# Ten gate and up pairs by seven products instead of nine, with the first pair's inputs and weight sums made earlier, in a two-layer encoder on one core

## The chip, the cores and the metric

The kernel runs on one core of one Trainium2 chip. TensorE (PE) multiplies, VectorE (DVE) and ScalarE (ACT) do elementwise work, GpSimd (POOL) issues accumulating transfers and takes powers, SyncE (SP) issues most other transfers. The time is the device time of one execution in microseconds, the median of several runs.

## The reference

Two layers over 512 tokens of 1024 channels, all in float32: layer 0 with latent attention, layer 1 with chunked attention over a shared key and value band. Each is followed by the feed-forward block that the change is about:

```python
def swiglu(h, w_gate, w_up, w_down):
    return (jax.nn.silu(h @ w_gate) * (h @ w_up)) @ w_down

for layer in range(DEPTH):
    h = rms_norm(x, attn_pre_g[layer])
    ...
    x = x + rms_norm(y, attn_post_g[layer])
    h = rms_norm(x, ffn_pre_g[layer])
    f = swiglu(h, ffn_w_gate[layer], ffn_w_up[layer], ffn_w_down[layer])
    x = x + rms_norm(f, ffn_post_g[layer])
```

`w_gate` and `w_up` are 1024 x 2816, `w_down` is 2816 x 1024.

## The kernel before, in words

**Halves.** Every float32 operand of a matmul is split into a high and a low half (`split`, L143: ScalarE casts the high half at L144, VectorE subtracts for the low half at L145), and each product is three matmuls: high by high, high by low, low by high. Weights arrive in `raw` buffers (512 KB, a ring of five) and their halves stand in `whi` and `wlo`, rings of three. `Feed` (L264) holds the plan of all weight pieces in order; `feed.next` hands out a piece and splits the next ones ahead.

**Blocks of the hidden layer.** The 2816 hidden units are 22 blocks of 128. A block's gate and up outputs stand transposed, hidden units on partitions and 512 tokens in the free dimension. The first `N_WHOLE` blocks, called whole units here, are multiplied plainly. Four whole units: the first two (weights `w_gu0`) in two halves of the tokens, so that they can begin while the second half of x is still made (`half`, L1153, four banks); units 2 and 3 (weights `w_gu`) on all 512 tokens by `proj` (L382, matmuls at L377 to L379).

**Pairs by seven products.** The other 18 blocks go in nine pairs (`products`, L1520, matmuls at L1550). For a pair, the weights of two blocks and two halves of the tokens make a 2 by 2 by 2 product, which is done with seven products instead of eight. Product j multiplies one of seven weight pieces (1024 columns: 4 quarters of the depth for gate and up) by one of seven moving operands of 256 tokens. Four of the seven pieces are sums of others, `raw[0]`, `raw[3]`, `raw[4]`, `raw[6]` (`Pair`, L151), made by accumulating transfers from POOL (L171) or by VectorE (L184). The moving operands are halves of x itself (`xs`, products 1, 2, 6) and sums of scaled x, here x-sums (`tb`, products 0, 3, 4, 5), made by `blocks_of` (L1315) once for all pairs. The results stand in the banks `be`, `al`, `ga` and are put together by ScalarE copies and VectorE adds; then the norm's factor (`rb`), silu (L1568) and the product with up follow.

**The order around it.** `ffn` (L1134) is the block: `out_proj` (L687) is the attention's output product, also in two halves of tokens; `Post.apply` (L667) adds the normed result to x, first half 0, then half 1 (y times a factor at L672, x plus y at L674, halves of x at L148 and L149). Behind each half stand its sums of squares for the next norm (`sx.squares`, L457 to L463), summed over channels by four transposing matmuls (L473). x of the layer is fetched ahead of `out_proj` (L683), and `mid` keeps x for later. In layer 1, `by_tokens` turns the result of layer 0 for the last stage, a piece in each of the products 0, 1, 3 and 5 from the second pair on. A scheduler puts each engine's instructions in order by dependences and by `behind` (issue after a named instruction) and `first` (priority); each engine then runs its queue strictly in order.

## Time and profile before

| | us |
|---|---|
| median of 3 runs | 1105.39 (1103.52 to 1105.41) |
| the profiled execution | 1105.07 |
| its span in the trace | 1103.3 |

The lines that matter are quoted in the prediction. In a line of the timeline the first number is the start in us from the begin of the span, the second how long it took, and in brackets stands the idle time before it and what ended that. In a group of instructions stand the count, the busy time in us, the mean of one in ns and the idle time just before. Names such as `whi<-raw` are output and input.

The costliest groups of the two elementwise engines:

```profile
L144 ACT CAST whi<-raw 128x1024 fp32r<-128x1024 f32 (+3 forms) x220 | 221.0, 1006 | 205.6 <-PE al L1550 71.5
L145 DVE TENSOR_TENSOR wlo<-raw,whi 128x1024 fp32r<-128x1024 f32 (+3 forms) x220 | 255.8, 1164 | 67.1 <-ACT whi L144 66.1
```

### The profile page before, as it was taken

How to read it: one execution, taken by the hardware profiler on the slowest of the kernel's cores; microseconds unless marked ns; L12 is line 12 of the kernel's file. 1: busy time of each engine (PE TensorE's matmuls, PEld its weight loads, DVE VectorE, ACT ScalarE, POOL GpSimd, SP SyncE). 2: the span in 40 equal slices, each digit the busy share in tenths (PEclk: the TensorE clock that was granted, in tenths of full speed). 3: DMA queues.
4: the chain of work that ended last, by engine and by line, in shares of the span. 5: the costliest groups of instructions: out<-in, count | busy, mean ns of one | idle time of the engine just before them, and what ended most of it. 6: DMA issues, size and time to landing. Idle time of an engine off the chain costs nothing.

```text
span 1103.3 us, 19079 instructions
## 1 busy us (share of the span) xinstructions
PE 1092.4 (99%) x6893; PEld 978.8 (89%) x6893; DVE 908.5 (82%) x1659; ACT 678.3 (61%) x1323; POOL 117.1 (11%) x181
## 2 busy tenths in 40 slices
PE   9999999999999999999999999999999999999997
PEld 6887889999999998888888888889899999998885
DVE  7787747988878889978858898758988889789977
ACT  7575737655555556668636767657645555556675
POOL 2211100101000001500000110000100010001401
PEclk9999999999999999999999999999999999999999
DMA  7344226447787757961555677634638888758913
GB/s 240 120 116 142 62 68 238 143 116 184 171 202 184 180 167 248 164 191 49 190 153 156 173 192 186 168 121 161 198 103 214 228 207 223 216 178 249 171 29 76
DMA packets 88334, 181.47 MB, mean 164 GB/s; under 512 B 26816, under 2 KB 28608, under 8 KB 88240
## 3 DMA queue, kind: packets, MB, share of 16 engines
q1 hardware_dynamic: 74752, 147.10, 43.1%
q0 software_dynamic: 13056, 32.73, 16.4%
q8 instruction: 54, 0.88, 0.3%
q10 hardware_dynamic: 432, 0.44, 0.1%
q14 instruction: 40, 0.33, 0.1%
HBM read 148.88 MB, written 10.88 MB: 145 GB/s over the span
## 4 chain that ended last, share of the span: by engine, by line
PE 97%; DVE 1%; ACT 1%; issue 1%; DMA 0%; POOL 0%; DVEq 0%; POOLq 0%; SPq 0%; ACTq 0%
PE al L1550 19%; PE b L377 11%; PE b L378 11%; PE b L379 11%; PE be L1550 9%; PE al L1306 8%; PE be L1306 5%; PE ga L1550 5%; PE de L1306 3%; PE ga L1306 3%; PE pt L561 2%; PE b L1707 2%; PE b L1107 1%; PE sc L1699 1%; PE sc L1698 1%
## 5 line engine op out<-in xcount | busy, mean ns | idle before, releaser
L144 ACT CAST whi<-raw 128x1024 fp32r<-128x1024 f32 (+3 forms) x220 | 221.0, 1006 | 205.6 <-PE al L1550 71.5
L145 DVE TENSOR_TENSOR wlo<-raw,whi 128x1024 fp32r<-128x1024 f32 (+3 forms) x220 | 255.8, 1164 | 67.1 <-ACT whi L144 66.1
L1550 PE MATMUL al<-th,whi 128*128 128x256 f32 x432 | 122.8, 284 | 0.0
L1550 PE MATMUL al<-th,wlo 128*128 128x256 f32 x432 | 121.0, 280 | 0.0
L1550 PE MATMUL al<-tl,whi 128*128 128x256 f32 x432 | 121.0, 280 | 0.0
L377 PE MATMUL b<-xh,whi 128*128 128x512 f32 x234 | 96.7, 415 | 0.0
L378 PE MATMUL b<-xl,whi 128*128 128x512 f32 x234 | 91.8, 392 | 0.0
L379 PE MATMUL b<-xh,wlo 128*128 128x512 f32 x234 | 91.7, 392 | 0.0
L1550 PEld LDWEIGHTS al<-th,whi 128*128 128x128 f32 x432 | 81.3, 188 | 2.2
L1550 PEld LDWEIGHTS al<-th,wlo 128*128 128x128 f32 x432 | 81.3, 188 | 0.2 <-DVE wlo L145 0.2
L1550 PEld LDWEIGHTS al<-tl,whi 128*128 128x128 f32 x432 | 81.3, 188 | 0.0
L548 ACT ACTIVATE p<-p,mn 128x128 f32<-128x128 f32 (+1 forms) x96 | 54.1, 563 | 36.0 <-DVE mn L546 34.1
L145 DVE TENSOR_TENSOR ptl<-pt,pth 128x128 fp32r<-128x128 f32 (+1 forms) x96 | 46.6, 485 | 30.5 <-ACT pth L144 29.6
L145 DVE TENSOR_TENSOR wlo<-wd,whi 128x512 fp32r<-128x512 f32 x86 | 56.3, 684 | 14.6 <-ACT whi L144 14.4
L144 ACT CAST whi<-wd 128x512 fp32r<-128x512 f32 x86 | 49.8, 618 | 25.0 <-PE al L1306 10.7
L144 ACT CAST pth<-pt 128x128 fp32r<-128x128 f32 (+1 forms) x96 | 40.3, 422 | 32.2 <-PE pt L561 31.3
L171 POOL DMA_DIRECT2D raw<-in_w_pair x32 | 28.1, 895 | 285.9 <-DVE ut L1562 84.1
L379 PEld LDWEIGHTS b<-xh,wlo 128*128 128x128 f32 x234 | 43.9, 188 | 9.9 <-DVE wlo L145 0.3
L1306 PE MATMUL al<-whi,pl 128*128 128x512 f32 x132 | 51.5, 390 | 0.0
L1306 PE MATMUL al<-wlo,ph 128*128 128x512 f32 x132 | 51.4, 389 | 0.0
L1306 PE MATMUL al<-whi,ph 128*128 128x512 f32 x132 | 51.4, 389 | 0.0
L377 PEld LDWEIGHTS b<-xh,whi 128*128 128x128 f32 x234 | 44.2, 189 | 5.7 <-ACT whi L144 0.2
(320 smaller groups left out, 3391.2 us busy)
## 6 DMA issues: line engine op xcount, KB each, us to landing
raw<-in_w_pair SPq DMA_DIRECT2D x88, 512.0 KB, 4.6
raw<-in_w_pair POOLq DMA_DIRECT2D x32, 512.0 KB, 7.6
wd<-in_w_down SPq DMA_DIRECT2D x54, 256.0 KB, 6.0
raw<-in_w_o SPq DMA_DIRECT2D x16, 512.0 KB, 4.0
raw<-in_w_gu SPq DMA_DIRECT2D x16, 512.0 KB, 4.7
raw<-in_w_down SPq DMA_DIRECT2D x16, 512.0 KB, 4.3
raw<-in_w_qkb SPq DMA_DIRECT2D x16, 512.0 KB, 3.5
wd<-in_w_down POOLq DMA_DIRECT2D x22, 256.0 KB, 5.0
```

The costliest lines, as they stand in the source:

```text
L144: return (nc.scalar.copy(dst_hi, src), V.tensor_tensor(dst_lo, src, dst_hi.bitcast(F32), op=OP.subtract))
L145: V.tensor_tensor(dst_lo, src, dst_hi.bitcast(F32), op=OP.subtract))
L171: nc.gpsimd.dma_start(r[j], self.src[n], accum_op=OP.add)
L377: nc.tensor.matmul(o, l[0], r[0], start=start, stop=False)
L378: nc.tensor.matmul(o, l[0], r[1], start=False, stop=False)
L379: last_mm[0] = nc.tensor.matmul(o, l[1], r[0], start=False, stop=stop)
L548: nc.scalar.activation(p[:, :n], p[:, :n], AF.Exp, bias=mn[:, :1], scale=-1.0, accum_out=self.sums[:, qt:qt + 1])
L561: nc.tensor.transpose(t[:, kt * P:(kt + 1) * P], p[:, kt * P:(kt + 1) * P], ident)
L1107: nc.tensor.matmul(o[:, q_], va[kt][:, part, v_], pt[:, kt, q_], start=n + kt == 0, stop=n == 2 and kt == NQT - 1)
L1306: nc.tensor.matmul(to[e], l[c], r[d], start=j < 4 and k == 0 and n == 0, stop=k == NF // 2 - 1 and n == 2, skip_group_check=True)
L1550: nc.tensor.matmul(o, l[c], r[d], start=first_ and n == 0, stop=k == K2 - 1 and n == 2, skip_group_check=True)
L1707: nc.tensor.matmul(o[:, q_], vv, pt[:, kt, q_], start=pt is pth and kt == 0, stop=pt is ptl and kt == NQT - 1)
```

## The change

`N_WHOLE` goes from 4 to 2: the whole units 2 and 3 and their weights `w_gu` go, and a tenth pair stands in their place, at the head of the pairs. The first pair now begins right behind the two whole units. Beside that:

- It runs its products in the order 1, 2, 0, 3, 6, 4, 5 (`FIRST_TURN`), those first that need no x-sum. Its matmuls are kept in that order by `behind(done)`. The first pair's add of `ga` comes after product 3.
- Its four weight sums are all made by accumulating transfers: `raw[0]` as before, and `raw[3]` and `raw[6]` from their own tiles by `chain`, each adding the one before it in SBUF. Its product 3 takes its halves from the ring `h`.
- `blocks_of` scales the first token half of x (`xg`) between the two halves of x, the second half with the x-sums; the x-sums of products 4 and 5 are made during products 0 and 3 and wait for the copies of product 0 (`at["ut"]`).
- The four banks of the whole units are copied to SBUF by ScalarE (`kept`, tiles named fu), so that the pair can use the banks.
- The sums of squares, the norm and its spread go into the second and third pair (`side`). Final gate work that has to wait for them is queued (`units`) and done from the third pair on, up to three gates in a pair.
- x is fetched at the end of the first half of `out_proj`, behind the loads of the next weights.
- In layer 1 the transposes of `by_tokens` stand from the sixth pair on, eight in each.

```diff
-N_WHOLE = 4
+N_WHOLE = 2
...
+    FIRST_TURN = (1, 2, 0, 3, 6, 4, 5)
...
         def begin(self):
 
-            r, self.made = self.raw, True
-            r[0] = r[3] = r[6] = self.tile(2, wide[0], "sum", 2)
+            r = self.raw
+            r[0] = self.tile(2, wide[0], "sum", 2)
+            if self.turn[0]:
+                r[3] = self.tile(0, wide[0], "sum", 2)
+                r[6] = self.tile(1, wide[0], "sum2", 2)
+            else:
+                r[3] = r[6] = r[0]
             r[4] = self.tile(2, wide[0], "sum2", 2)
-            for j, n in ((0, 3), (4, 0)):
-                with tc.issue_after(last_pow[0].ins):
-                    nc.gpsimd.dma_start(r[j], self.src[n], accum_op=OP.add)
+            self.add(0, self.src[3])
+            self.add(4, self.src[0])
+
+        def add(self, j, src):
+            with tc.issue_after(last_pow[0].ins):
+                nc.gpsimd.dma_start(self.raw[j], src, accum_op=OP.add)
+
+        def chain(self):
+
+            self.add(3, self.raw[0])
+            self.add(6, self.raw[3])
...
             if not h:
                 feed.ahead(2 if late else 3)
+                feed.loaded = get_x(feed.loads[feed.pos + (4 if late else 5)])
...
         rest = half(0)
         post.apply(x, 0, sx.each)
         post.add_half(1, last, rest, 9, 14)
+        tb, hid = [], Hidden(H)
+        more = blocks_of(x, G_FPRE[i], H, tb)
+        with behind(feed.behind[len(feed.ready)][1]):
+            next(more)
         run(rest)
-        sx.squares(0)
-        post.apply(x, 1, sx.each)
+        base = feed.pos
+        pair = feed.plan[base][0]
+        pair.chain()
+        feed.behind[base + 2] = feed.behind[base + 3] = post.apply(x, 1, sx.each)
+        next(more)
+        feed.ahead(3)
         run(half(1))
-        sx.squares(1)
...
-        b = [bank(), bank()]
-        rest = proj(2, KT, 4, xs, b)
...
+        kept = [H(name="fu") for _ in banks]
+        for t, b in zip(kept[:2], banks[:2]):
+            nc.scalar.copy(t, b)
+        with behind(next(more)[0]):
+            for t, b in zip(kept[2:], banks[2:]):
+                empty = nc.scalar.copy(t, b)
...
+        def step():
+            feed.lows[base + 4] = next(more)[1]
+            feed.split(base + 4)
+
+        def step_():
+            for n in (5, 6):
+                with behind(at["ut"]), behind(feed.low):
+                    feed.lows[base + n] = at["t"] = next(more)[1]
+                if n == 5:
+                    feed.split(base + 5)
+
+        side = {(0, 2): step, (0, 3): step_, (1, 1): lambda: sx.squares(0),
+                (1, 4): lambda: sx.squares(1), (1, 6): norm, (2, 2): spread_}
+        units = [lambda f=f: gate(*kept[2 * f:2 * f + 2]) for f in range(N_WHOLE)]
...
+        done = mm = None
         for p in range(pairs):
...
-            for j in range(7):
-                if aside is not None and p and j in (0, 1, 3, 5):
+            for j in (range(7) if p else FIRST_TURN):
+                if (p, j) in side:
+                    side[p, j]()
+                if p > 1 and j in ((3, 5) if p == 2 else (1, 3, 5)) and units:
+                    units.pop(0)()
+                for _ in range(1 + (j == 3) if aside is not None and p > 4 else 0):
                     next(aside, None)
                 w = feed.next(1024, 2)
+                done = None if p else mm
...
                     else:
                         V.tensor_tensor(t[:, A1], t[:, A1], o, op=OP.add)
-                        V.tensor_tensor(t, t, rb, op=OP.mult)
...
+                        units.append(lambda t=t, u=u: gated(t, u))
+                        while p > 6 and units:
+                            units.pop(0)()
```

Three places of the new order, by engine. **TensorE, from product 4 to product 5 of the first pair in layer 0**; `be_635` or `al_651` are banks, `whi_653` the high half of a weight piece. Before, the last matmuls of product 4 and then product 5:

```order
L1550 MATMUL al_651_2912<-th_585_2620,whi_653_2942 128x256
L1550 MATMUL al_651_2912<-tl_586_2621,whi_653_2942 128x256
L1550 MATMUL al_651_2912<-th_585_2620,wlo_654_2943 128x256
L1550 MATMUL al_650_2911<-th_573_2608,whi_658_2976 128x256 [waits DVE_49]
L1550 MATMUL al_650_2911<-tl_574_2609,whi_658_2976 128x256
L1550 MATMUL al_650_2911<-th_573_2608,wlo_659_2977 128x256
```

Now, from the end of product 4 (`whi_618`); `whi_622` belongs to product 0 and `whi_626` to product 1 of the second pair, `whi_620` to product 5:

```order
L1606 MATMUL al_611_2679<-tl_580_2494,whi_618_2778 128x256
L1606 MATMUL al_611_2679<-th_579_2493,wlo_619_2779 128x256
L1606 MATMUL be_628_2910<-th_565_2479,whi_622_2844 128x256 [waits Activation_49]
L1606 MATMUL be_628_2910<-tl_566_2480,whi_622_2844 128x256
L1606 MATMUL be_629_2911<-th_565_2479,whi_622_2844 128x256
L1606 MATMUL be_629_2911<-tl_566_2480,whi_622_2844 128x256
L1606 MATMUL al_647_2976<-xh_532_2263,whi_626_2880 128x256 [waits DVE_49,Activation_49]
L1606 MATMUL be_628_2910<-th_565_2479,wlo_623_2845 128x256 [waits DVE_49]
L1606 MATMUL be_628_2910<-th_569_2483,whi_622_2844 128x256
L1606 MATMUL be_628_2910<-tl_570_2484,whi_622_2844 128x256
L1606 MATMUL al_610_2678<-th_567_2481,whi_620_2814 128x256 [waits DVE_49]
```

Product 5, which stood right behind product 4, now stands behind eight matmuls of the next pair, one of them of its product 1, whose high half takes the buffer of `whi_618`, the third before it in the ring. The order of layer 1 is the same at this place.

**VectorE, in the later products of a pair.** Before, in the second pair of layer 0, from the low half of product 4 (`wlo_689`) on to that of product 6:

```order
L145 TENSOR_TENSOR wlo_694_3227<-raw_647_2904,whi_693_3226 128x1024 [waits DMAHW2_49,Activation_49]
L145 TENSOR_TENSOR wlo_696_3258<-raw_641_2864,whi_695_3257 128x1024 [waits PE_49,Activation_49]
L1562 TENSOR_TENSOR ut_678_3123<-al_685_3162,ut_678_3123 128x256 [waits PE_49]
L1562 TENSOR_TENSOR ut_679_3124<-al_686_3163,ut_679_3124 128x256 [waits PE_49]
L145 TENSOR_TENSOR wlo_698_3288<-raw_664_3067,whi_697_3287 128x1024 [waits DMASW5_49,Activation_49]
```

Now, in the third pair of the ten, from the low half of product 4 (`wlo_692`) to that of product 6 (`wlo_700`); `fu` are the copied banks, `gt` gates of the first two pairs, `bc` the spread norm:

```order
L146 TENSOR_TENSOR wlo_692_3280<-raw_625_2876,whi_691_3279 128x1024 [waits DMASW1_49,PE_49,Activation_49]
L1616 TENSOR_TENSOR gt_677_3201<-gt_677_3201,ga_693_3283 128x256 [waits PE_49]
L1215 TENSOR_TENSOR fu_600_2647<-fu_600_2647,bc_689_3275 128x512 [waits Activation_49]
L1215 TENSOR_TENSOR fu_602_2649<-fu_602_2649,bc_689_3275 128x512
L1616 TENSOR_TENSOR gt_678_3202<-gt_678_3202,ga_694_3284 128x256 [waits PE_49]
L1569 TENSOR_TENSOR gt_606_2674<-gt_606_2674,bc_689_3275 128x512
L1569 TENSOR_TENSOR gt_607_2675<-gt_607_2675,bc_689_3275 128x512
L1218 SCALAR_TENSOR_TENSOR hd_695_3313<-fu_600_2647,fu_601_2648 128x512 [waits Activation_49]
L1569 TENSOR_TENSOR gt_630_2912<-gt_630_2912,bc_689_3275 128x512
L146 TENSOR_TENSOR wlo_698_3318<-raw_644_2969,whi_697_3317 128x1024 [waits DMAHW2_49,Activation_49]
L1569 TENSOR_TENSOR gt_631_2913<-gt_631_2913,bc_689_3275 128x512
L146 TENSOR_TENSOR wlo_700_3349<-raw_624_2874,whi_699_3348 128x1024 [waits DVE_49,PE_49,Activation_49]
```

Seven multiplies of the queued gate work now stand among these splits. On TensorE, three matmuls of product 6 of this pair (`whi_699`, `wlo_700`) stand ahead of its product 5.

**VectorE, ahead of the second half of x in layer 1.** Before, from the first fence of the norm on:

```order
L644 COPY f_1805_9063<-r_1804_9061 128x2 [waits Pool_49]
L145 TENSOR_TENSOR wh_1808_9089<-raw_1755_8819,wh_1807_9088 128x512 [waits DMAHW1_49]
L145 TENSOR_TENSOR wlo_1817_9132<-raw_1760_8829,whi_1816_9131 128x1024 [waits DMAHW2_49]
L149 SCALAR_TENSOR_TENSOR xl_1799_9018<-x_1718_8636,gains_70,xh_1798_9017 128x256 [waits Activation_49]
L145 TENSOR_TENSOR wh_1810_9091<-raw_1755_8819,wh_1809_9090 128x512 [waits Activation_49]
L145 TENSOR_TENSOR wlo_1869_9393<-raw_1806_9086,whi_1868_9392 128x1024 [waits DMAHW3_49]
L459 SCALAR_TENSOR_TENSOR acc_1818_9159<-acc_1818_9159,sq_1819_9161 128x256 [waits Activation_49]
L145 TENSOR_TENSOR wlo_1875_9434<-raw_1812_9123,whi_1874_9433 128x1024 [waits DMAHW4_49]
L672 TENSOR_TENSOR y_1726_8686<-y_1726_8686,bc_1811_9117 128x256 [waits PE_49]
```

Now:

```order
L657 COPY f_1828_9208<-r_1827_9206 128x2 [waits Pool_49]
L146 TENSOR_TENSOR wh_1830_9232<-raw_1760_8926,wh_1829_9231 128x512
L146 TENSOR_TENSOR wlo_1843_9283<-raw_1761_8928,whi_1842_9282 128x1024
L150 SCALAR_TENSOR_TENSOR xl_1822_9163<-x_1783_8972,gains_70,xh_1821_9162 128x256 [waits Activation_49]
L146 TENSOR_TENSOR wh_1832_9234<-raw_1760_8926,wh_1831_9233 128x512 [waits Activation_49]
L146 TENSOR_TENSOR wlo_1869_9385<-raw_1766_8938,whi_1868_9384 128x1024 [waits DMAHW7_49]
L688 TENSOR_TENSOR y_1735_8801<-y_1735_8801,bc_1833_9260 128x256 [waits PE_49]
```

A sum of squares and a split that stood ahead of y's multiply are gone from there.

More of the change, by code (lines that the diff above doesn't have):

```diff
@@ L140, in first, with split @@
         tc.cur_priority += n
-    def split(dst_hi, dst_lo, src):
-        return (nc.scalar.copy(dst_hi, src),
-                V.tensor_tensor(dst_lo, src, dst_hi.bitcast(F32), op=OP.subtract))
+    def split(dst_hi, dst_lo, src, after=None):
+        hi = nc.scalar.copy(dst_hi, src)
+        with behind(after):
+            return hi, V.tensor_tensor(dst_lo, src, dst_hi.bitcast(F32), op=OP.subtract)
     def split_scaled(dst_hi, dst_lo, src, col):
@@ L268, in __init__ @@
             self.plan, self.raw, self.ready, self.pos, self.room = [], [], [], 0, {}
-            self.behind, self.gate, self.low = {}, None, None
+            self.behind, self.gate, self.low, self.loads, self.lows = {}, None, None, {}, {}
         def add(self, src, n, gain=None, room=None):
@@ L296, in load @@
                 if isinstance(src, Pair):
-                    src.load(j)
+                    self.loads[len(self.raw)] = src.load(j)
                     self.raw.append(None)
@@ L644, in add_half @@
                 fence = V.tensor_copy(small("f")[:, :v.shape[1]], r),
+            if not h:
+                with behind(feed.loaded):
+                    next(p for p, *_ in feed.plan[feed.pos:] if isinstance(p, Pair)).begin()
             for n in range(len(feed.ready), len(feed.ready) + 6):
@@ new lines, in ffn, with norm, spread_, gate @@
+        with behind(next(more)[0]):
+            for t, b in zip(kept[2:], banks[2:]):
+                empty = nc.scalar.copy(t, b)
+        eps = sp.tile([P, 4], F32, tag="eps", name=f"eps_{i}", bufs=1)
+        rb = []
+        def norm():
+            v = sx.sum.total(None, 300)
+            with first(300):
+                r = rstd(v)
+            V.tensor_scalar(eps, v, EPS, None, op0=OP.mult)
+            rb.append(r)
+        def spread_():
+            rb[0] = spread_sb(rb[0])
+        def gate(t, u):
+            V.tensor_tensor(t, t, rb[0], op=OP.mult)
```

146 lines of the change are left out of this document (67 added, 79 removed).

## The prediction

> **What bounds the kernel now.** I read the page first, for which engine sets the end, then the matmuls one after the other at the edges of the stage that the change rewrites, then the other engines in that stage.
>
> ```profile
> span 1103.3 us, 19079 instructions
> PE 1092.4 (99%) x6893; PEld 978.8 (89%) x6893; DVE 908.5 (82%) x1659; ACT 678.3 (61%) x1323; POOL 117.1 (11%) x181
> PEclk9999999999999999999999999999999999999999
> PE 97%; DVE 1%; ACT 1%; issue 1%; DMA 0%; POOL 0%; DVEq 0%; POOLq 0%; SPq 0%; ACTq 0%
> ```
>
> TensorE is busy 99% of the span, and 97% of the chain that ended last is TensorE, at the full granted clock throughout. So a matmul less is worth its whole spacing, provided that no new wait comes in its place. VectorE's 82% says that such a wait would most likely come from there. The timeline of TensorE gives the spacings and the edges of the gate and up stage (start, duration):
>
> ```profile
> 212.07 0.40 PE L377 MATMUL b<-xh,whi 128*128 128x512 f32 x1
> 214.14 0.60 PE L473 MATMUL tot<-ident,acc 128*128 128x128 f32 x4
> 214.49 0.48 PE L377 MATMUL b<-xh,whi 128*128 128x512 f32 x1
> 234.82 0.28 PE L1550 MATMUL be<-th,whi 128*128 128x256 f32 x1
> 414.49 0.39 PE L1306 MATMUL al<-whi,ph 128*128 128x512 f32 x1
> 787.20 0.40 PE L377 MATMUL b<-xh,whi 128*128 128x512 f32 x1
> 809.92 0.28 PE L1550 MATMUL be<-th,whi 128*128 128x256 f32 x1
> 989.79 0.40 PE L1306 MATMUL al<-whi,ph 128*128 128x512 f32 x1
> ```
>
> In layer 0 the two whole units that the change turns into a pair run from 212.07 to 234.82, the nine pairs from there to 414.49; in layer 1 it is 787.20, 809.92 and 989.79. From 212.07 to 214.14 there are nine matmuls of 512 columns, 0.230 us each. How full the engines are beside them, by stretches:
>
> ```profile
> core 0: us, PE busy (x) PEld busy (x) DVE busy (x) ACT busy (x) POOL busy (x), PEclk, DMA share, GB/s
> 195.00:212.00 17.00, 17.00 (x144) 17.00 (x144) 17.00 (x43) 10.66 (x23) 0.00 (x0) 1.00 0.54 187
> 212.00:235.00 23.00, 23.00 (x108) 19.05 (x108) 20.85 (x43) 13.91 (x24) 2.90 (x3) 1.00 0.38 92
> 235.00:255.00 20.00, 20.00 (x171) 19.87 (x171) 16.65 (x24) 11.02 (x18) 0.86 (x1) 1.00 0.58 159
> ```
>
> VectorE has no room at all just ahead of the stage (17.00 of 17.00), about 2 us in the stretch that is replaced, and over 3 us in each pair.
>
> **Part 1, the pair itself.** The two whole units are 96 matmuls of 512 columns: 96 x 0.230 = 22.05 us. The stretch is 22.75 us long, since eight small transposes stand in it, four from 214.14 to 214.49 and as many for the spread of the norm; both groups stay, moved into the next pairs. A pair is 168 matmuls of 256 columns, and nine take 414.49 - 234.82 = 179.67 us, or 19.97 us each (0.119 us a matmul). In layer 1 it is (989.79 - 809.92) / 9 = 19.99. So the exchange is worth 22.05 - 19.97 = 2.08 us in each layer, **4.16 us** in both, as long as TensorE never waits.
>
> The Trainium skill, in TensorE: Matmul & The Clock Gate, section Back-to-back issue gap, gives an isolated gap of N/2.4 + 2.5 ns at the warm clock, which is 216 ns for 512 columns and 109 ns for 256. An estimate by that page is 96 x 0.216 - 168 x 0.109 = 2.4 us a layer. The rows of this trace are longer at both sizes (230 and 119 ns) and decide.
>
> **Part 2, the hand-over in the first pair.** The first pair runs its products as 1, 2, 0, 3, 6, 4, 5, at 2.85 us each, so from 212.07 product 4 starts at 226.3 and product 5 at 229.2. The order of TensorE in the changed kernel puts four matmuls of the next pair's product 0 behind product 4, then one of its product 1, and product 5 only after these. That one matmul reads a high half that takes the same one of three buffers as product 4's. What such a reuse costs, a product of before shows, first in TensorE's rows, then in ScalarE's, with the group of weight loads last:
>
> ```profile
> 240.21 0.28 PE L1550 MATMUL al<-xl,whi 128*128 128x256 f32 x1
> 240.33 0.28 PE L1550 MATMUL al<-xh,wlo 128*128 128x256 f32 x1
> 240.45 0.28 PE L1550 MATMUL ga<-xh,whi 128*128 128x256 f32 x1
> ...
> 240.59 1.05 ACT L144 CAST whi<-raw 128x1024 fp32r<-128x1024 f32 x1 [0.97 <-PE al L1550]
> ...
> L1550 PEld LDWEIGHTS al<-th,whi 128*128 128x128 f32 x432 | 81.3, 188 | 2.2
> ```
>
> The last matmul of a product starts at 240.33, and the cast into the buffer that it frees runs from 240.59 to 241.64: 1.3 us after that start. Before, a whole other product (2.85 us) stood in between. Now only four matmuls do: the reader is due 5 x 0.119 = 0.6 us after the start of product 4's last, and gets its data 1.3 us after it. That leaves 0.7 us of waiting, and a weight load of 0.19 that can't begin sooner. I take **0.8 us in each layer**; the order is the same in layer 1. The bounds are 0.5 (the cast starts at the last reader of the high half, a matmul earlier) and 1.2 (ScalarE is in another instruction when the buffer comes free).
>
> **Part 3, gates in the third pair.** The final gate work of the whole units and of the first pairs waits for the norm, which the change makes in the second pair. It then stands in VectorE's queue in the third. Of two products in that pair TensorE takes three matmuls of product 6 ahead of product 5, so it needs product 6's low half as early as product 5's. VectorE has in its queue, from product 4's low half up to product 6's, three splits of 1024, seven multiplies of 512 and two adds of 256 columns.
>
> ```profile
> L145 DVE TENSOR_TENSOR wlo<-raw,whi 128x1024 fp32r<-128x1024 f32 x194 | 236.4, 1220 | 65.7 <-ACT whi L144 65.1
> L1567 DVE TENSOR_TENSOR gt<-gt,bc 128x512 f32<-128x512 f32 x36 | 24.9, 692 | 1.2
> L1562 DVE TENSOR_TENSOR ut<-al,ut 128x256 f32<-128x256 f32 x36 | 15.1, 421 | 8.2 <-PE al L1550 8.2
> ```
>
> Back to back these overlap by some 0.08 us, so they cost 1.14, 0.61 and 0.34: 3 x 1.14 + 7 x 0.61 + 2 x 0.34 = 8.4 us. The split that begins it waits for a cast of 1.05 us that is due when product 1 ends, so it starts 1.3 us after that end, and the last low half is there 9.7 us after it. TensorE asks for it after three products, four transposes and two matmuls: 3 x 2.85 + 0.35 + 0.24 = 9.15. I take **0.4 us in each layer**, less than the difference because the first split can start a little early; the bounds are 0 and 1.2.
>
> **Part 4, the second half of layer 1.** Before, TensorE loses time there, on its timeline and VectorE's:
>
> ```profile
> 774.81 0.28 PE L379 MATMUL b<-xh,wh 128*128 128x256 f32 x1
> 775.32 0.50 PE L377 MATMUL b<-xh,wh 128*128 128x256 f32 x2 [0.22 <-ACT xh L148]
> 775.84 0.39 PE L378 MATMUL b<-xl,wh 128*128 128x256 f32 x1
> ...
> 772.17 0.41 DVE L459 SCALAR_TENSOR_TENSOR acc<-acc,sq 128x256 f32<-128x256 f32 x1
> 772.51 1.22 DVE L145 TENSOR_TENSOR wlo<-raw,whi 128x1024 fp32r<-128x1024 f32 x1
> 773.64 0.74 DVE L672 TENSOR_TENSOR y<-y,bc 128x256 f32<-128x256 f32 x2
> ```
>
> Three matmuls take from 774.81 to 775.84 where 0.36 us would do: 0.6 us are lost, because y's multiply (L672) starts at 773.64 behind a sum of squares and a split. Both are gone from that place in the new order, 1.47 us of VectorE, so x is there before it is asked for. I take a gain of **0.5 us**, once; bounds 0 and 0.6.
>
> **Part 5, what I cost at nothing.** The x-sums of the first pair are the tightest. Before, VectorE begins with x-sums at 209.63, and eleven sums of squares (six in the row ahead) stand between these and x; gone, they let it begin 11 x 0.34 = 3.7 us earlier, at 205.9. Up to the last x-sum of the pair there are then 36 instructions in its queue: 27 of 256 columns, 6 of 512 and 3 of 1024, or 27 x 0.34 + 6 x 0.61 + 3 x 1.14 = 16.3 us, up to 222.2 without a wait. But the last two are told to wait for the copies of product 0, which end near 221.2, and go from VectorE to ScalarE and back each time. What that takes, the same sums show in before:
>
> ```profile
> 207.62 2.09 DVE L463 TENSOR_TENSOR acc<-acc,sq 128x256 f32<-128x256 f32 x6
> 209.63 0.41 DVE L1326 TENSOR_TENSOR t<-xg 128x256 f32<-128x256 f32 x1
> ...
> 227.19 0.41 DVE L1338 TENSOR_TENSOR t<-xg,xg 128x256 f32<-128x256 f32 x1
> 234.48 0.68 DVE L145 TENSOR_TENSOR tl<-t,th 128x512 fp32r<-128x512 f32 x1
> ```
>
> Four of them end at 235.16, 8 us in all with two long instructions among them. Two such, with a split and an add of the pair, are 5 to 6 us, so the last is there near 227.0. Product 4 reads it from 227.5 on (226.3 and ten matmuls): hidden, with half a microsecond to spare.
>
> The sums of weights come by accumulating transfers, three in a row from POOL:
>
> ```profile
> 193.10 0.80 POOL L483 TENSOR_TENSOR r<-ss,mhalf 128x2 f32<-128x2 f32 x1 [10.71 <-DVE ss L476]
> raw<-in_w_pair POOLq DMA_DIRECT2D x32, 512.0 KB, 7.6
> wd<-raw POOLq DMA_DIRECT2D x22, 256.0 KB, 4.1
> 162.87 4.65 SPq L683 DMA_DIRECT2D x<-in_x  x8
> 168.20 10.15 SPq L303 DMA_DIRECT2D raw<-in_w_gu  x6
> ```
>
> The first lands about the time of the power at 193.10 on the same queue, and two more at 7.6 us and an issue of 0.9 give 202 and 211; sources in SBUF are no slower (4.1 us for half the size). Product 6 starts at 223.5 and needs its sum by 222, so 11 us are spare. The eight x transfers of layer 0 now stand on SP behind loads that in before went out between 168.20 and 178.35, one for each buffer that came free; I expect them out from about 176 on and landed by 186, while the last half of the output product still runs. If they are late, TensorE waits in layer 0 alone, a microsecond for each. Twelve more issues on POOL (11% busy) and eight copies of banks on ScalarE (13.91 of 23.00 us busy in that stretch) fall into free time.
>
> **The sum.** -4.16 + 2 x 0.8 + 2 x 0.4 - 0.5 = -2.26 us. The profiled execution took 1105.07 us, of which 1103.3 are span, so 1102.8; the median of the runs is 1105.39, 0.3 above it, so **1103.1 us**.
>
> **Rivals.** First, **no new waits**: if the cast and the gates are in time, -4.16 and up to -0.6 leave 1100.7. For it speaks that the old order showed almost no wait in a pair; against it the three buffers. Second, **the gates eat the rest**: from the third pair to the seventh there are three gates a pair for two, two multiplies more, which raise VectorE from 16.65 to 17.9 us of 19.97; in layer 1 the transposes for the next stage come later and twice as dense, eight a pair. If each such pair loses 0.2 us, that is 2 us over both layers, 1105.1. Against it: 2 us of room. Third, **the first pair starves, and it is slower**. The place is the last x-sum and product 4. It decides at 227.5: if the copies of product 0 come later than 221.7, each microsecond is lost twice, once in each layer. ScalarE stands in order ahead of them with weight casts and bank copies; were it behind by two casts and a copy (2.5 us), and product 5's split behind it too by the same, that is 3 us a layer with the slack taken off, 1109. Against it speaks ScalarE's free third. Fourth, **the pairs are not what limits**: if what the exchange saves comes back as a wait where the down product begins (414.49), the time stays 1105.4; in before TensorE passes that point without a wait, so I give it little.
>
> The granted clock is full in all 40 slices, so a wait costs its own length here. The Trainium skill, in TensorE: Matmul & The Clock Gate, section What's actually happening, has the clock halve after an idle window of about 3.4 us; by that rule the third rival would cost up to 1.7 us more in each layer, as an estimate, and no wait of this trace is long enough to show it.
>
> **How the numbers follow.** Forecast 0.47 (1101.9 to 1104.5), no new waits 0.18, gates 0.15, starving 0.12, nothing gained 0.05, the rest beyond. What a measurement of this kernel can tell from no change is about 0.2%, 2.2 us, so the forecast lies on the line of 1103.2 and is split in half. Faster: 0.24 + 0.18 + a little = 0.45; same: 0.23 + 0.15 + 0.04 = 0.42; slower 0.13. The range runs from the no-wait case with its full gain to 1.1 us above the case of the gates, 1100.6 to 1106.2, and leaves out the starving case.
>
> **What would show it.** Right: TensorE's first wait of the stage, 0.7 to 0.9 us, is between product 4 and product 5 of the first pair, near 230 and 805, released by a cast; a second, of under 1 us, lies in the third pair, released by a low half; the ten pairs are 199.7 us of matmuls plus these; the wait at 775 is gone. Wrong: a wait ahead of product 0 or 4 released by an x-sum, waits in the fourth to the tenth pair, or TensorE waiting for x ahead of 212.

## The result and the profile after

| | before | after |
|---|---|---|
| median of 7 runs, us | 1105.35 (1103.52 to 1105.41) | 1107.89 (1106.34 to 1112.25) |
| profiled execution, its span, us | 1105.07, 1103.3 | 1107.97, 1106.2 |

The ratio is 1.0031, with a 95% interval of 1.0016 to 1.0046: the change makes the kernel slower, by 2.5 us in the medians, where 2.3 us faster was forecast. The page of after, the lines on the engines:

```profile
span 1106.2 us, 19445 instructions
PE 1091.0 (99%) x7037; PEld 984.0 (89%) x7037; DVE 912.0 (82%) x1675; ACT 694.0 (63%) x1371; POOL 129.2 (12%) x193
```

The page tells little: TensorE 99% and VectorE 82% as before, ScalarE 63% for 61%. What changed shows at the edges of the stage. TensorE's timeline of after, at the first matmul of the first pair and the first of the down product, layer 0 and then layer 1:

```profile
212.58 0.28 PE L1606 MATMUL al<-xh,whi 128*128 128x256 f32 x1
416.03 0.40 PE L1337 MATMUL al<-whi,ph 128*128 128x512 f32 x1
788.08 0.28 PE L1606 MATMUL al<-xh,whi 128*128 128x256 f32 x1
992.10 0.40 PE L1337 MATMUL al<-whi,ph 128*128 128x512 f32 x1
```

The stage took 203.45 us in layer 0 and 204.02 in layer 1; before it was 414.49 - 212.07 = 202.42 and 989.79 - 787.20 = 202.59. So the two stages lose 2.46 us where 1.8 were to be won. Between the two stages 0.66 us were won (372.05 for 372.71). The rest of the span's 2.9 us is a start later by 0.5 and a tail longer by 0.6. The start is late by 0.5 in the attention already, ahead of all that the change touches; why the tail is longer stays open. What TensorE waited for (line, releaser: us in all, times, longest), first from 205 to 420 us; `whi` and `wlo` are the high and low half of a weight piece, `tl` the low half of an x-sum, and `ut` is VectorE's add of product 4:

```profile
PE al L1606 <- ACT whi L144: 0.6, 1, 0.6
PE al L1606 <- DVE ut L1623: 0.4, 1, 0.4
PE al L1606 <- DVE tl L146: 0.3, 1, 0.3
PE be L1606 <- DVE wlo L146: 0.3, 1, 0.3
```

and from 780 to 995 us:

```profile
PE al L1606 <- DVE ut L1623: 0.8, 2, 0.6
PE al L1606 <- ACT whi L144: 0.6, 1, 0.6
PE be L1606 <- DVE wlo L146: 0.3, 1, 0.3
PE al L1606 <- DVE wlo L146: 0.2, 1, 0.2
```

Before, both lists are empty within the stage. In each list two of the rows were forecast (`ACT whi` and `be <- DVE wlo`), the others not. These are idle times only; what a wait costs is read from the starts of the matmuls, against a spacing of 0.119 us. Where the waits are, on TensorE's timeline of after:

```profile
228.08 0.39 PE L1606 MATMUL al<-th,whi 128*128 128x256 f32 x1
228.81 0.39 PE L1606 MATMUL al<-tl,whi 128*128 128x256 f32 x1 [0.34 <-DVE tl L146]
...
230.92 0.28 PE L1606 MATMUL be<-tl,whi 128*128 128x256 f32 x1
231.79 0.38 PE L1606 MATMUL al<-xh,whi 128*128 128x256 f32 x1 [0.60 <-ACT whi L144]
...
250.43 0.39 PE L1606 MATMUL al<-th,whi 128*128 128x256 f32 x1 [0.38 <-DVE ut L1623]
...
899.40 0.38 PE L1606 MATMUL al<-th,wlo 128*128 128x256 f32 x1 [0.21 <-DVE wlo L146]
...
905.88 0.39 PE L1606 MATMUL al<-th,whi 128*128 128x256 f32 x1 [0.59 <-DVE ut L1623]
```

From 230.92 to 231.79 are 0.87 us, so 0.75 are lost, and some 0.1 to 0.3 more in the one or two matmuls behind a wait, which come slower. Summed in this way, with those after-effects, in us:

| place | layer 0 | layer 1 | forecast, each layer |
|---|---|---|---|
| first pair, product 4: last x-sum | 1.02 | 0 | 0 |
| first pair, hand-over to product 5: cast | 1.02 | 0.87 | 0.8 |
| second pair, product 5: VectorE's add of product 4 | 0.65 | 0.50 | 0 |
| third pair, product 6: low half | 0.58 | 0.58 | 0.4 |
| sixth to eighth pair: low half, adds | 0 | 1.60 | 0 |
| sum | 3.27 | 3.55 | 1.2 |

With the exchange at 2.08 us a layer and no wait the stage would take 200.34 and 200.51 us; with these sums it is 203.61 and 204.06, within 0.2 of what it took. The agreement is a little too good: a pair of before, too, loses some 0.19 us at the first two matmuls of product 5, and the 19.97 us of a pair hold that already. Without it the rows come to about 2.7 and 2.6 us, so 0.4 and 0.9 us are in no row; stretches in which the spacing is 0.1188 us where it is 0.1176 in others make up part of that. Within this the exchange brought what it should, and waits beyond those forecast, 3 or 4.4 us by the two ways of counting, ate it.

**Why the last x-sum is late in layer 0.** The timeline of after, POOL's three accumulating transfers for the first pair, then ScalarE, then VectorE:

```profile
191.75 0.96 POOL L182 DMA_DIRECT2D raw<-in_w_pair  x1 [8.85 <-ACT xh L149]
200.30 0.92 POOL L182 DMA_DIRECT2D raw<-raw  x1 [6.13 <-DMA raw<-in_w_pair]
209.59 0.88 POOL L182 DMA_DIRECT2D raw<-raw  x1 [7.47 <-DMA raw<-raw]
...
219.22 1.05 ACT L144 CAST whi<-raw 128x1024 fp32r<-128x1024 f32 x1 [3.98 <-DMA raw<-raw]
...
221.09 1.29 DVE L146 TENSOR_TENSOR tl<-t,th 128x512 fp32r<-128x512 f32 x2 [4.32 <-ACT th L144]
```

Each transfer is issued when the one before it has landed; from one issue to the next, and from the last to the cast, are 8.6, 9.3 and 9.6 us, and ScalarE had the last one's data at 219.22. That is still ahead of product 6. But the cast of that sum stands in ScalarE's queue ahead of the casts of the x-sums (`th`), and ScalarE stood still for 3.98 us on it; VectorE then stood 4.32 us, and everything behind it came late, up to the x-sum of product 4 at 228.

**Why pairs six to eight wait in layer 1.** SyncE's and VectorE's timeline of after:

```profile
890.53 0.48 SPq L1250 DMA_DIRECT2D x<-mid  x1
...
892.75 0.69 DVE L1569 TENSOR_TENSOR gt<-gt,bc 128x512 f32<-128x512 f32 x1
897.53 0.71 DVE L1253 STREAM_TRANSPOSE xt<-x 128x512 f32<-128x512 f32 x1 [4.09 <-DMA x<-mid]
```

A piece takes three steps of `by_tokens`: ask for its transfer, transpose it, write it out. The eight a pair are such steps, not eight transposes; there are eight transposes in all. With two steps in product 3 of the sixth pair, a piece is asked for at 890.53 and its transpose is put into VectorE's queue in the same product. The transfer landed 7.0 us later, VectorE stood 4.09 us, and the low half behind it was late for TensorE at 899.40; the transposes of 0.7 us are not what costs.

**Why the second pair waits.** VectorE's timeline of after:

```profile
249.62 0.42 DVE L476 TENSOR_TENSOR acc<-acc,sq 128x256 f32<-128x256 f32 x1
249.96 0.42 DVE L1623 TENSOR_TENSOR ut<-al,ut 128x256 f32<-128x256 f32 x1
```

Products 4 and 5 add onto the same bank `al`, and VectorE must read what product 4 left before product 5 may write. That add stands behind sums of squares, which the change moved here, and a split between them; TensorE goes on at 250.43, when it is done.

### The profile page after: what moved, and what is told of

It is laid out like the page before. It is cut to its first block, busy times and chain, and to the rows that moved or that the text cites. A ratio compares the mean times of both kernels' runs of the same rounds, so it can differ in the third digit from the quotient of the medians.

```text
span 1106.2 us, 19445 instructions
## 1 busy us (share of the span) xinstructions
PE 1091.0 (99%) x7037; PEld 984.0 (89%) x7037; DVE 912.0 (82%) x1675; ACT 694.0 (63%) x1371; POOL 129.2 (12%) x193
## 5 line engine op out<-in xcount | busy, mean ns | idle before, releaser
L1606 PE MATMUL al<-th,whi 128*128 128x256 f32 x464 | 132.1, 285 | 1.4 <-DVE ut L1623 1.2
L1606 PE MATMUL al<-tl,whi 128*128 128x256 f32 x464 | 130.2, 281 | 0.3 <-DVE tl L146 0.3
L1606 PE MATMUL al<-th,wlo 128*128 128x256 f32 x464 | 130.1, 280 | 0.2 <-DVE wlo L146 0.2
L1606 PEld LDWEIGHTS al<-tl,whi 128*128 128x128 f32 x464 | 87.4, 188 | 0.5 <-DVE tl L146 0.5
L390 PE MATMUL b<-xh,whi 128*128 128x512 f32 x170 | 71.7, 422 | 0.0
L182 POOL DMA_DIRECT2D raw<-in_w_pair x40 | 35.5, 904 | 282.7 <-DMA raw<-in_w_pair 116.8
L392 PE MATMUL b<-xh,wlo 128*128 128x512 f32 x170 | 66.8, 393 | 0.2 <-DVE wlo L146 0.2
L391 PE MATMUL b<-xl,whi 128*128 128x512 f32 x170 | 66.7, 393 | 0.0
L1606 PE MATMUL al<-xh,whi 128*128 128x256 f32 x160 | 45.0, 282 | 1.2 <-ACT whi L144 1.2
L1606 PE MATMUL be<-xh,wlo 128*128 128x256 f32 x160 | 45.0, 281 | 0.6 <-DVE wlo L146 0.6
```

The lines of the kernel that those rows point to most:

```text
L182: nc.gpsimd.dma_start(self.raw[j], src, accum_op=OP.add)
L390: nc.tensor.matmul(o, l[0], r[0], start=start, stop=False)
L391: nc.tensor.matmul(o, l[0], r[1], start=False, stop=False)
L392: last_mm[0] = nc.tensor.matmul(o, l[1], r[0], start=False, stop=stop)
L1606: mm = nc.tensor.matmul(o, l[c], r[d], start=first_ and n == 0, stop=k == K2 - 1 and n == 2, skip_group_check=True)
```

## The experiments

All are edits of the changed kernel. Each has 4 to 11 runs, of which the median is given, and beside them runs of the kernel before; the ratio, with its 95% interval, is that of all runs to those, and need not be the ratio of two medians. Medians of two experiments compare only to about 1 us, since the kernel before had medians from 1104.43 to 1105.35.

**e1_strict: the order of the first pair kept for all pairs**, so that no matmuls of the next pair come ahead of product 5.

```diff
-                done = None if p else mm
+                done = mm
```

> The changed kernel with one edit: every product's matmuls are kept behind the last matmul of the product before, in all pairs and not in the first alone. The theory that each wait of TensorE costs its own length says that the waits between products 4 and 5 of the first pair (0.76 + 0.16 + 0.11 us in layer 0, 0.76 + 0.11 in layer 1) and in the third pair (0.48 + 0.10 in each layer) go and nothing comes in their place: about 2.5 us less than the changed kernel, near 1105.4. The rival, that VectorE is behind anyway and TensorE waits for it a little later, says 1107 to 1108 and waits of the same sum at the next product. A second rival, that the 1.1 us which the changed kernel lost outside the stage (0.5 at the start, 0.6 at the end of the trace) belong to it, is seen in any of these profiles: it says that they are there each time.

1111.07 us, ratio 1.0059 (1.0044 to 1.0074): slower still. From 205 to 420 us, the list of waits, and TensorE's timeline at the hand-over:

```profile
PE al L1606 <- DVE ut L1623: 3.2, 5, 1.7
PE al L1606 <- DVE tl L146: 0.3, 1, 0.3
```

```profile
229.98 0.28 PE L1606 MATMUL al<-th,wlo 128*128 128x256 f32 x1
231.93 0.39 PE L1606 MATMUL al<-th,whi 128*128 128x256 f32 x1 [1.66 <-DVE ut L1623]
```

The cast is out of the list, and 1.83 us are lost to VectorE's add of product 4 instead (from 229.98 to 231.93 are 1.95). So the eight early matmuls are not what the hand-over costs: they cover about half of a wait that lies deeper. The other four waits for `ut` stand in later pairs, which have lost the same cover.

**e2_squares: the sums of squares two and one products earlier.**

```diff
-        side = {(0, 2): step, (0, 3): step_, (1, 1): lambda: sx.squares(0),
-                (1, 4): lambda: sx.squares(1), (1, 6): norm, (2, 2): spread_}
+        side = {(0, 2): step, (0, 3): step_, (1, 0): lambda: sx.squares(0),
+                (1, 2): lambda: sx.squares(1), (1, 6): norm, (2, 2): spread_}
```

> The changed kernel with one edit: the sums of squares are called at products 0 and 2 of the second pair and not at 1 and 4. The theory is that TensorE's wait at product 5 of the second pair (0.54 + 0.11 us in layer 0, 0.39 + 0.11 in layer 1) is for the second add of product 4, which stands in VectorE's queue behind sums of squares and a split of weights; with the two adds next to one another it goes: 1.1 us less than the changed kernel, near 1106.8. The rival, that VectorE has too much work in that pair whatever its order, says that the wait comes elsewhere in the pair with the same length, and 1107.9.

1106.21, ratio 1.0020 (1.0010 to 1.0030). The second pair's waits are gone in both layers; the hand-over still loses 1.05 and 0.78 us, released by a low half (`be <- DVE wlo`) and no longer by the cast. The profiled execution, 1109.33, was the longest of the ten; its timeline shows what the doubled step can cost, VectorE and then TensorE:

```profile
899.37 0.71 DVE L1253 STREAM_TRANSPOSE xt<-x 128x512 f32<-128x512 f32 x1 [6.41 <-DMA x<-mid]
...
901.24 0.38 PE L1606 MATMUL al<-th,wlo 128*128 128x256 f32 x1 [2.52 <-DVE wlo L146]
```

The same transfer took 9.3 us where it took 7.0 in after, and TensorE stands 2.52 us in place of 0.21.

**e3_x_early: x fetched ahead of the output product again.**

```diff
-        x = []
+        fetch(x_src, x := [])
...
-        last = out_proj(osp, KT, post, firsts, 2, late, lambda after: fetch(x_src, x, after))
+        last = out_proj(osp, KT, post, firsts, 2, late, lambda after: after)
```

> The changed kernel with one edit: x is fetched at the start of the block again, ahead of the last six loads of weights. The theory is that the late fetch put the loads of the first pair's weight sums, and with these the three accumulating transfers, 8 us late in layer 0 (the third landed at 219.1), that ScalarE stood 4.0 us in front of the cast that needs it, and that the last x-sums and product 4 came late by this: TensorE's 0.30 + 0.61 + 0.11 us at 228 go, 1.0 us less than the changed kernel, near 1106.9, and the third transfer lands some us earlier. The rival, that the x-sums are slow by their own chain between VectorE and ScalarE (they wait for the copies of product 0), says that ScalarE's wait goes and TensorE's stays, 1107.9.

1106.51, ratio 1.0014 (1.0005 to 1.0024). Its timeline on POOL and ScalarE:

```profile
183.04 0.96 POOL L182 DMA_DIRECT2D raw<-in_w_pair  x1 [1.64 <-ACT y L634]
...
197.93 0.88 POOL L182 DMA_DIRECT2D raw<-raw  x1 [4.38 <-DMA raw<-raw]
...
214.03 1.05 ACT L144 CAST whi<-raw 128x1024 fp32r<-128x1024 f32 x1 [0.28 <-ACT gt L1613]
```

The last sum goes out 12 us earlier, ScalarE no longer stands for it, and the wait at product 4 is gone. The one at the hand-over is not (0.75 us and what follows). The runs that leave x late say the same: where that cast of ScalarE stood 3.23, 3.38, 3.74, 3.98 and 4.06 us (e4, e11, e1, after, e2), TensorE lost 0.28, 0.43, 0.78, 1.02 and 1.09 us at product 4.

**e4_tokens: one transpose in a product, from the fourth pair on.**

```diff
-                for _ in range(1 + (j == 3) if aside is not None and p > 4 else 0):
+                if aside is not None and p > 2 and j in (0, 1, 3, 5):
```

> The changed kernel with one edit: the transposes of layer 1 begin in the fourth pair, one step in each of the products 0, 1, 3 and 5, and never two in one product. The theory is that with two steps at product 3 a transpose stands in VectorE's queue right behind the issue of its own transfer, and VectorE stood 4.1 us for it at 893.4: TensorE's waits at 899, 905 and 944 (0.37 + 0.10, 0.75 + 0.11, 0.27 us) go, 1.6 us less than the changed kernel, near 1106.3. The rival, that VectorE has too much to do with three gates in a pair, says that waits of about that sum stay in the sixth to the eighth pair, 1107.9, or come in the fourth and fifth, where the transposes go.

1108.46, ratio 1.0043 (1.0029 to 1.0057): no gain. The waits at 899 to 944 are gone, but the last transfer of x was issued at 977.84 and landed at 982.73, VectorE stood 2.6 us for it, and TensorE lost 4.3 us at three places from 984 to 999. By this the place was wrong and not the cause; e11 settles it.

**e5_three: the edits of e2 and e3, and transposes from the third pair on, together.**

```diff
-                for _ in range(1 + (j == 3) if aside is not None and p > 4 else 0):
+                if aside is not None and p > 1 and j in (0, 1, 3, 5):
```

> Three edits of the changed kernel at once: the sums of squares at products 0 and 2 of the second pair, x fetched early, and the transposes spread one step at a time from the third pair on (products 0, 1, 3, 5), so that the last is over two pairs before the end. By the theory that the waits are separate, each with its own cause, the waits at 228 (1.0 us), at 250 and 824 (0.65 and 0.5) and those of the transposes (1.6) go together, 3.7 us less than the changed kernel's 1107.9: near 1104.2, at the time of the kernel before. The two waits left in each layer are those that were forecast, after product 4 of the first pair (0.9 to 1.0 us) and in the third pair (0.6). The rival that VectorE as a whole is the bound from the third to the eighth pair says 1106 or more, with waits in these pairs.

1108.08 (1104.28 to 1110.03), ratio 1.0022 (1.0009 to 1.0035). Three edits that each take a wait away don't give their sum: the hand-over is still there (0.78 in both layers), and in layer 1 waits for `ut` come in the fourth and sixth pair (0.76 us at 863, 0.61 at 904), where transposes now stand among the gates; that these are the cause is not shown.

**e6_first: the last x-sums at the start of the pair** (with e3 and the transposes of e5; squares at products 1 and 2), and **e7_gates: e6, and queued gates only behind the low half in hand**.

```diff
-                with behind(at["ut"]), behind(feed.low):
+                with behind(feed.low):
...
-        side = {(0, 2): step, (0, 3): step_, (1, 1): lambda: sx.squares(0),
+        side = {(0, 2): step, (0, 0): step_, (1, 1): lambda: sx.squares(0),
```

and, in e7 alone,

```diff
-                    units.pop(0)()
+                    with behind(feed.low):
+                        units.pop(0)()
```

> As e5_three, and the last two x-sums of the first pair are called at product 0 and no longer wait for the copies of product 0, so that VectorE makes them in the 3 us in which it stood (at 219 to 222 in e3_x_early); the sums of squares are called at products 1 and 2 of the second pair. The theory since e1_strict: what TensorE really lacks behind product 4 of the first pair are VectorE's adds of product 4, behind two splits, since product 5 adds onto the same bank; the matmuls of the next pair only fill the gap as far as their own buffers let them. With VectorE 2 to 3 us earlier the wait of 0.9 to 1.0 us goes in both layers, and TensorE takes product 5 right behind product 4: 1102.3. The rival, that the cast into the buffer of product 4 (0.8 us) is what is lacked and has nothing to do with VectorE, says that the wait stays as long, 1104.2.

> As e6_first, and each queued gate is put behind the newest low half in VectorE's queue, so that the gate work of the first two pairs no longer stands ahead of the splits of products 5 and 6 in the third pair. The theory says that TensorE's wait in the third pair (0.48 + 0.10 us in each layer) goes and the gates find room later: 1101.1, which is the exchange of matmuls (4.16) with almost no wait, about 3.5 us under the kernel before. The rival says that VectorE, at 19 of 20 us in the fourth and fifth pair, has no room for gates that come later, and waits of the same sum come there or in the last pairs: 1102.3 or more.

1108.81, ratio 1.0035 (1.0022 to 1.0047), and 1107.02, ratio 1.0024 (1.0014 to 1.0034). The wait at the hand-over is gone, and another has come ahead of product 6, 1.02 us in each layer in e6, released by ScalarE's copies of product 0, which now stand behind the casts of the x-sums. More waits, of 0.6 to 1.3 us, come in the second pair and in layer 1. The x-sums must be neither late nor first. In e7 the third pair's wait falls from 0.48 to 0.35 only.

**e8_lows: e2 and e3, and the low halves of products 4 and 5 not tied to the x-sums**; transposes in products 0, 3 and 5 from the second pair on.

```diff
-                    feed.lows[base + n] = at["t"] = next(more)[1]
+                    at["t"] = next(more)[1]
...
-                for _ in range(1 + (j == 3) if aside is not None and p > 4 else 0):
+                if aside is not None and p and j in (0, 3, 5):
```

> e6_first showed that product 6 waits for the copies of product 0 (same bank), so the x-sums stay behind these copies, as in e5_three. New edit: the low halves of products 4 and 5 are no longer told to wait for the last x-sums, so that VectorE makes them in the 3 us in which it stands for ScalarE; squares at products 0 and 2 of the second pair, x early, and the transposes one for each pair from the second on (products 0, 3 and 5). The theory: with these two splits (2.3 us) out of the way VectorE's adds of product 4 come right behind the product, TensorE has no wait left in the first pair of either layer (0.78 + 0.1 us each in e5_three), and with one transpose in a pair those of 0.77 and 0.61 us at 863 and 903 go as well; left is the third pair, 0.5 us a layer. Against the profile of e5_three (1105.5) that is 3.1 us less, 1102.4. The rival, that VectorE's total work in the first two pairs is what lacks, says that the wait moves into the second pair: 1104.5 to 1105.5.

1105.59, ratio 1.0006 (0.9997 to 1.0015). The first and second pair have no wait at all in either layer: with the low halves made as the weights come, VectorE reaches product 4's add in time, and the eight matmuls of the next pair no longer stand ahead of product 5. What is left, from 780 to 1000 us, and VectorE's timeline at the last transpose:

```profile
PE be L1606 <- DVE wlo L146: 1.7, 2, 1.3
PE al L1337 <- ACT ph L144: 1.5, 1, 1.5
PE al L1337 <- ACT whi L144: 0.6, 1, 0.6
```

```profile
979.25 0.71 DVE L1253 STREAM_TRANSPOSE xt<-x 128x512 f32<-128x512 f32 x1 [2.25 <-DMA x<-mid]
```

Three steps a pair end too late: the last transpose meets its transfer in the tenth pair. **e9_all**, e8 with the gates of e7, was slower:

> As e8_lows, with each queued gate behind the newest low half in VectorE's queue, as in e7_gates, where this left 0.35 us of 0.48 in the third pair because the second add of product 4 stands behind a multiply. The theory of separate waits says a gain of 0.3 us over e8_lows, 1102.1; the rival of VectorE's total work says no gain or a loss from the sixth pair on, 1102.4 to 1104.

1106.83, ratio 1.0022 (1.0013 to 1.0032). The end of layer 1's stage waits again (1.85 us up to 985.99, 1.49 up to 999.32), and what the gates gain in the third pair is 0.05 and 0.11 us.

**e10_best: e8 with the transposes of before**, and **e11_tokens: that edit alone on the changed kernel**.

```diff
-                for _ in range(1 + (j == 3) if aside is not None and p > 4 else 0):
+                if aside is not None and p and j in (0, 1, 3, 5):
```

> The kernel of e8_lows with the transposes for the last stage as before the change: one in each of products 0, 1, 3 and 5 of the second to the seventh pair. In the profile of e8 the last transpose stood behind its transfer and TensorE waited 0.72, 1.52 and 1.64 us between 980 and 996. Theory of separate waits, each with a cause and a place of its own: with the transposes early again these 3.9 us go, the first two pairs stay free of waits, and the time is e8's median of 1105.6 less 3 to 4: 1101.5 to 1102.6, faster than before the change by 2 to 3 us. Rival, VectorE as a whole is the bound (19.3 to 19.7 of 20 us busy in the pairs with three gates): the transposes in the third to seventh pair meet the gates there, 2 to 4 us of small waits come back in those pairs, and the time is 1104 to 1106.

> The changed kernel with one edit undone: the transposes for the last stage as before the change, one in each of products 0, 1, 3 and 5 of the second to the seventh pair. Theory that two transposes in one product, each behind its own transfer, cost layer 1 its waits at 899, 905 and 944 (0.37, 0.75 and 0.27 us, with the 0.1 that goes with each): those are gone, all else stays, and the time is 1107.9 less 1.4 to 1.7, about 1106.3. Rival, VectorE as a whole is the bound: waits of the same size come in the third to fifth pair of layer 1, 1107.5 to 1108.5.

e10: **1102.41** (1100.39 to 1103.66), ratio **0.9980** (0.9972 to 0.9989), faster than the kernel before by 2.0 us; the changed kernel was slower than it by 2.5. e11: 1105.20 (1103.47 to 1106.65), ratio 1.0005 (0.9996 to 1.0014). Waits of e10 from 780 to 1000 us, and its edges on TensorE's timeline:

```profile
PE be L1606 <- DVE wlo L146: 0.2, 1, 0.2
```

```profile
212.28 0.28 PE L1606 MATMUL al<-xh,whi 128*128 128x256 f32 x1
413.33 0.39 PE L1337 MATMUL al<-whi,ph 128*128 128x512 f32 x1
785.33 0.28 PE L1606 MATMUL al<-xh,whi 128*128 128x256 f32 x1
986.98 0.40 PE L1337 MATMUL al<-whi,ph 128*128 128x512 f32 x1
```

The stages take 201.05 and 201.65 us, 0.7 and 1.1 us over the time with no wait at all. In the fifth pair of layer 1, with transposes and three gates, the busy times of e10 are:

```profile
867.00:887.00 20.00, 20.00 (x170) 19.84 (x168) 19.94 (x32) 10.85 (x18) 1.71 (x2) 1.00 0.89 221
```

VectorE is busy for 19.94 of 20 us, TensorE for all 20. So the rival, that VectorE as a whole is the bound, falls: the only wait left in e10's stage is that of the third pair, 0.4 us in each layer. In e11 layer 1's stage falls from 204.02 to 202.26, 1.8 us for the 1.4 to 1.7 expected. Its median lies 0.8 us above the kernel before's beside it, where the changed kernel's lay 2.5 above, so that 1.8 us went there too.

**e12_gate: e10 with one gate in the third pair for two.**

```diff
-                if p > 1 and j in ((3, 5) if p == 2 else (1, 3, 5)) and units:
+                if p > 1 and j in ((5,) if p == 2 else (1, 3, 5)) and units:
```

> The kernel of e10_best with one final gate in the third pair in place of two: the first of the two whole units' products (0.6 us on VectorE, L1218) leaves the place between product 4's and product 6's low halves. In e10's profile VectorE has that product at 263.71 and the low half of product 6 ends at 267.87, for which TensorE waits 0.37 and 0.1 us in each layer. Theory that VectorE's queue there is the whole cause: 0.6 us less in it is more than the 0.48 that was waited, the wait is gone in both layers, and the time is 1102.4 less 0.9, about 1101.5, with no TensorE wait over 0.2 us left in the stage. Rival: the gate that is put off meets a pair where VectorE is busy 19.0 to 19.9 of 20 us, and a wait of 0.4 to 0.6 us comes in the fourth to sixth pair: 1102.0 to 1102.8.

1103.24, ratio 0.9980 (0.9971 to 0.9989): no gain over e10. The product `hd` kept its place, at 264.21 ahead of the two low halves, since the scheduler put the one gate that was left there; layer 0 loses 0.36 us as in e10 (0.37). So the edit didn't take away what it was meant to, and the cause of the third pair's wait remains argued from the queue. In layer 1 a transpose slipped in there, ahead of its transfer (VectorE, then TensorE):

```profile
840.00 0.71 DVE L1253 STREAM_TRANSPOSE xt<-x 128x512 f32<-128x512 f32 x1 [1.21 <-DMA x<-mid]
...
843.62 0.38 PE L1606 MATMUL be<-xh,wlo 128*128 128x256 f32 x1 [1.60 <-DVE wlo L146]
```

## Why the prediction was wrong

- **Part 1, right.** The spacing in the pairs stayed 0.119 us, and in e10, with nearly all waits gone, the stages come to 201.05 and 201.65 us for the 200.34 and 200.51 that the 2.08 us a layer give; some 0.5 us of the rest in each layer are the third pair's wait.
- **Part 2, the size right (1.02 and 0.87 for 0.8), in part by luck, since the reason was half right.** The wait was released by the cast into the reused buffer, as forecast. But e1 shows that without this reader the add of product 4 holds product 5 back 1.8 us. e8 took both away by freeing the low halves from the x-sums; the order of TensorE was the symptom.
- **Part 3, right**: 0.58 with its after-effect, for 0.4, in both layers. That the seven multiplies alone make it was not shown.
- **Part 4, right**: no wait at 775, and 0.66 us won between the stages for 0.5.
- **The signs of being wrong came.** The prediction named a wait ahead of product 4 released by an x-sum, and waits in the fourth to the tenth pair; both are in the lists (`tl` at 228.81, and 899 to 944).
- **Part 5, wrong, and with it the forecast.** It is the part that cost things at nothing, and three of them failed:
  - "so 11 us are spare" for the weight sums. The first transfer, taken to land at 193, was only issued at 191.75, since its inputs had been pushed back by the fetch of x (with x early, in e3, it goes out at 183.04); the last landed 8 us late. The slack was counted to product 6, the reader on TensorE. The nearest reader in a strict queue was ScalarE, whose cast of that sum stands ahead of the x-sums' casts: it stood still from 215.2 on. With it "hidden, with half a microsecond to spare" fell. e3 shows it: x early, and this wait is gone. It was the third rival's consequence, by another road than ScalarE's load.
  - The sums of squares, moved into the second pair, were priced only by what they free ahead of the stage. Where they now stand they delay the add of product 4: 0.65 and 0.50 us (e2 takes it away).
  - The transposes of layer 1, 1.6 us in this profile, were seen as denser work, in the second rival, and its eight transposes a pair are eight steps. What costs is that a transfer no longer has a product or more to land in before its transpose (e11 takes this away, 1.8 us).
- **The second rival's other half, too low**: VectorE's load with three gates a pair was put at 17.9 us. The busy times in after, with columns as in the prediction's table of stretches:

```profile
272.00:292.00 20.00, 20.00 (x171) 19.87 (x170) 19.69 (x31) 10.88 (x18) 1.75 (x2) 1.00 0.79 189
292.00:312.00 20.00, 20.00 (x169) 19.87 (x168) 19.29 (x32) 10.94 (x18) 1.74 (x2) 1.00 0.76 191
```

  VectorE is at 19.69 and 19.29 of 20 us, and yet TensorE doesn't wait in these two stretches (20.00 of 20.00). A full VectorE cost nothing here, as what TensorE needed stood early in its queue. The prediction added two multiplies for the third gate and left out the adds of hidden blocks for the down product (`hs`, 256 columns) that come with it: nine of them stand in the first of these stretches, and four in the 20 us from 275 of before.
- **The clock, misread, without weight in the sum.** The prediction took from 40 slices at full clock that a wait costs its own length, and that no wait of this trace could show more. A slice is 27.6 us long and hides a drop of some 4 us; the last section shows one, in before itself, behind a wait of 1.92 us.

The sum by its own terms, with the figures of the table: -4.16 held; the stalls of 2.4 became 1.02 + 0.87 + 0.58 + 0.58 = 3.05 where they were forecast, and 1.02 + 1.15 + 1.60 = 3.77 came where none was. So the step that failed is the nothing set for the moved work in part 5.

## What to carry to other kernels

When work moves into a stage, follow each moved instruction to the next thing behind it in the same queue, not only to the engine that reads its result: here a late sum, a sum of squares and a transpose each hurt work that doesn't depend on them. A transfer should be asked for well ahead of the instruction that waits for it, in an in-order queue above all: here one took 5 to 9 us to land, two to three products. And a change that seems to lose may hold its gain: when the waits were listed by place and cause and undone, the same exchange came out at 0.998 of the time before.

## What the runs showed of the hardware

A wait of 2 us can cost a second time. In the attention of layer 0, outside the change, TensorE waits 1.92 us in before and in e8 alike. TensorE's timeline of before there, and its busy times and granted clock (the last but two) in the stretch behind it, then those of e8:

```profile
106.67 0.50 PE L1094 MATMUL sc<-kh,qh 128*128 128x128 f32 x2 [1.92 <-ACT kh L144]
```

```profile
107.00:112.00 5.00, 5.00 (x23) 4.75 (x23) 4.24 (x11) 2.31 (x7) 1.05 (x2) 0.66 0.71 258
```

```profile
107.00:112.00 5.00, 4.30 (x26) 3.80 (x27) 4.86 (x12) 3.26 (x9) 1.05 (x2) 1.00 0.86 286
```

In before the granted clock falls to 0.66 over these 5 us, in e8 it stays at 1.00. The code there is the same, and by the starts of the matmuls, beside those of e3, the drop costs 1.2 to 1.4 us. It fell in twelve of the fourteen profiles, and not in those of e3 and e8. The same came behind the 2.52 us wait of e2 (0.66 from 901 to 906) and the one of 1.85 us in e9 (0.66 from 985 to 990), and in the gate and up stages behind no wait of up to 1.69 us (1.00 from 987 to 992 in e4, from 231 to 236 in e1). So some of the scatter between runs may be this. The Trainium skill, in TensorE: Matmul & The Clock Gate, section What's actually happening, has the clock halve after an idle window of about 3.4 us and says that the window is free-running. The second agrees with one wait having two outcomes; for the first, waits of 1.85 to 2.52 us were enough here.
